# The z projection of a state-space block: two head groups in one product of 512 columns, in every second group

## The chip, the cores and the metric

The kernel runs on one core of one Trainium2 chip. The metric is the device time of one execution in microseconds (us), smaller is better. The times of this kernel of three runs lie within 0.13% of each other.

## The reference, cut to what matters

One transformer-like block on 512 tokens of width 1024, in float32. The input is normalised to `h`; one large projection `h @ w_in` gives the convolution branch, `z`, the state-space inputs `x`, `B`, `C`, the step sizes and the gates. What concerns us is the state-space branch, cut into 8 groups of 4 heads (256 of the 2048 columns of `z` belong to each group):

```
z   = proj[..., OFF_Z:OFF_XBC]                 # 2048 columns, 256 to a group
xbc = silu(causal_depthwise_conv(xbc, ...))    # x, B, C of every group
y   = ssd_chunked(x, dt, a, B, C, d_skip)      # the scan over chunks
y   = y * silu(z)
yg  = y by group;  yg = yg * rsqrt(mean(yg*yg) + eps)
ssm_out = (yg * norm_g) @ out_w
```

After it come the gates, an output projection, a residual, and a gated feed-forward layer.

## The kernel before, in words

Every float32 product is made in three passes. A factor is split into a rounded half `hi` and a remainder `lo`, and `mm3` (L160) issues hi*hi, hi*lo and lo*hi into one PSUM tile, so every logical product is three matmul instructions on TensorE (L162, L163, L164). The halves of `h` (`hhi`, `hlo`) stay in SBUF for the whole branch. The weights come in strips of 128 x 1024 values, in the order that the list `ORDER` writes out by hand (L84 to L97). A strip is loaded by SyncE's queue into one of five `raw` tiles, cast by ScalarE into `whi` (L129), and its remainder `wlo` is made either by VectorE (L134) or, for every second position in the list, by ScalarE's negated copy and an accumulating DMA that GpSimd issues (L131, L132). There are five `whi`/`wlo` slots; `w_get` asks for the strip that is needed and the three after it.

The branch runs in a loop over the groups g = 0..7 (L622 to L647). In a group the program issues: the two x products `proj_x` (24 matmuls of 512 columns each), then `s4(g-2)` (transposes of a finished y, tiles `pyT`, `yh`, `yl`) and `s1(g-1)` (transposes `pxT` and `pBT`, the product `pcb`), the B product, in odd groups from g = 3 half of the output projection `ssm_out` (`pso`), `s2(g-1)` (states `pSa`, `pSb`, and `yd`), the C product, the other half of `ssm_out`, `s3(g-1)`, and `proj_z(g)`. Then the decay table `L` of the next group is made: a DMA, a mask on GpSimd, 16 exponentials on ScalarE. In this text a group with even g is an even group, one with odd g an odd group; only odd groups (from 3) hold the 96 matmuls of `ssm_out`.

`s3(g)` is the step that uses z: it adds the parts of y (L558, L575), with the products `pYa`, `pYb` (L562) between them, multiplies by z (L577), squares on ScalarE (L582), takes the power on GpSimd (L170) and scales y on VectorE (L585). `s4(g)` one group later needs that result.

`proj_z` (L484) has the tokens as the stationary operand: for each of four chunks of 128 tokens and 8 steps in depth it issues three matmuls of 256 columns, 96 in all, two token chunks to one PSUM tile; ScalarE turns each full tile into z by one SiLU of 512 values to a partition (L496). The z of group 0 is made earlier together with the step sizes (`proj_z0`). z lives in one tile (tag `z`, one buffer), the projections share three PSUM tiles (tag `mm`).

VectorE also carries the long convolution of the other branch: 240 multiply-adds ("taps", L390), a share of which is released after each product (`conv_some`), never ahead of the last product issued. After the loop come the gates: `gate("gs", 0..4)` with `s4(6)`, `s1(7)`, `s2(7)`, `s3(7)`, `s4(7)` in between, each gate's sigmoid written to a tile of the ring `sg` (five buffers, idle during the group loop), and the last part of `ssm_out`.

The order on each engine is not quite that of the program: a planner at build time places each instruction by its own estimate of when operands and tiles come free, earlier program order first, so that a step whose operands it takes to be late is slipped between products of a later step. At run time every engine keeps the planned order.

Of the kernel before, what the change touches and what calls it, by code (L numbers as in the profile page):

```python
# [10 lines left out]
F32 = mybir.dt.float32  # L11
F32R = mybir.dt.float32r
BF16 = mybir.dt.bfloat16
AF = mybir.ActivationFunctionType
ALU = mybir.AluOpType
# [3 lines left out]
P = 128  # L19
T = 512  # L20
NT = T // P
D = 1024
NK = D // P
# [3 lines left out]
G = 8  # L27
HG = H // G
GW = DI // G
# [38 lines left out]
W_AHEAD = 3  # L68
# [7 lines left out]
DMA_EVERY = 2  # L76
DMA_FROM = 8
# [6 lines left out]
ORDER = []  # L84
# [3 lines left out]
for _g in range(G):  # L88
    _so = [("so", 2 * _g - 6 + _i) for _i in range(4)] if _g % 2 and _g > 1 else []
    ORDER += [("x", 2 * _g), ("x", 2 * _g + 1), ("B", _g)] + _so[:2] + [("C", _g)] + _so[2:]  # L90
    ORDER += [("z", 2 * _g), ("z", 2 * _g + 1)] if _g else []
ORDER += [("gs", _i) for _i in range(5)] + [("so", 2 * G - 4 + _i) for _i in range(4)]
ORDER += [("gs", _i) for _i in range(5, NK)] + [("gc", _i) for _i in range(NK)] + [("pw", _i) for _i in range(NK)]
ORDER += [("wo", _i) for _i in range(NK)]
ORDER += [("gu", 2 * _i) for _i in range(EARLY_U)] + [("gu", 2 * _i + 1) for _i in range(EARLY_U)]
ORDER += [("gu", _i) for _i in range(2 * EARLY_U, 2 * NF)]
ORDER += [("wd", _i) for _i in range(NF)]  # L97


def b3(ap, n):  # L100
# [5 lines left out]
def block_kernel(ctx: ExitStack, tc: tile.TileContext, x, xT, prm, hp, gp, w, out):  # L106
    nc = tc.nc
    act, dve, pe, pool = nc.scalar, nc.vector, nc.tensor, nc.gpsimd
# [11 lines left out]
    seq = {key: n for n, key in enumerate(ORDER)}  # L120
# [6 lines left out]
    def w_part(n, c):  # L127
        (hi, lo), src = split[n], raws[n]
        act.copy(hi[:, c], src[:, c])  # L129
        if n % DMA_EVERY == DMA_EVERY - 1 and DMA_FROM < n < seq[("gs", 0)]:  # L130
            act.activation(lo[:, c], hi[:, c].bitcast(F32), AF.Copy, scale=-1.0)  # L131
            pool.dma_start(lo[:, c], w[n][:, c].bitcast(F32R), accum_op=ALU.add)  # L132
        else:
            dve.tensor_tensor(out=lo[:, c], in0=src[:, c], in1=hi[:, c].bitcast(F32), op=ALU.subtract)  # L134
# [8 lines left out]
        if parts == 1:  # L143
            w_part(n, slice(0, 1024))

    def w_get(*key):

        n = seq[key]
        for m in range(n, n + W_AHEAD + 1):
            w_split(m)  # L150
        return split[n]

# [34 lines left out]
    hhi = hp_pool.tile([P, NK, T], F32R, tag="hi", name="hhi")  # L187
# [26 lines left out]
    def mm_tile(name):  # L214
        return mmp.tile([P, T], F32, tag="mm", name=name)
# [16 lines left out]
    ps = aux_tile("warm_ps")  # L232
# [163 lines left out]
    st = {}  # L396
# [84 lines left out]
        proj(ps, w_get(n, g))  # L481
        st[g][n] = conv4(ps, (2 if n == "B" else 3) * G + g, f"{n}{g}")

    def proj_z(g):  # L484
        z = ssd.tile([P, NT, GW], F32, tag="z", bufs=1, name=f"z{g}")
        ws = [w_get("z", 2 * g + j) for j in range(2)]
        for t2 in range(2):
            ps = mm_tile(f"pz{g}_{t2}")
            for t in range(2):
                tok = slice((2 * t2 + t) * P, (2 * t2 + t + 1) * P)  # L490
                o = ps[:, t * GW : (t + 1) * GW]
                for k in range(NK):
                    wh, wl = ws[k // 4]
                    c = slice((k % 4) * GW, (k % 4 + 1) * GW)
                    mm3(o, hhi[:, k, tok], hlo[:, k, tok], wh[:, c], wl[:, c], k == 0, k == NK - 1)
            act.activation(z[:, 2 * t2 : 2 * t2 + 2, :], ps.rearrange("p (a b) -> p a b", a=2), AF.Silu)  # L496
        st[g]["z"] = z

    def s1(g):
        s = st[g]  # L500
# [52 lines left out]
    def s3(g):  # L553
        s = st[g]
        hs = slice(HG * g, HG * (g + 1))
        y = s["y"]
        for n in range(2):
            dve.tensor_tensor(out=y[:, 2 * n : 2 * n + 2], in0=s["yd"][n], in1=y[:, 2 * n : 2 * n + 2], op=ALU.add)  # L558
        pa, pb = aux_tile(f"pYa{g}"), aux_tile(f"pYb{g}")
        pY = [None, pa[:, :GW], pa[:, GW:], pb[:, :GW]]  # L560
        for c in range(1, NT):
            pe.matmul(  # L562
                pY[c], s["C"][:, c * P : (c + 1) * P], s["prev"][:, c - 1].rearrange("p h d -> p (h d)"),
                start=True, stop=True,
            )
        yo = ssd.tile([P, NT - 1, HG, HD], F32, tag="yo", name=f"yo{g}")
        dve.tensor_tensor(
            out=yo[:, 0:2], in0=pa.rearrange("p (c h d) -> p c h d", c=2, h=HG),
            in1=b3(eacs[:, 1:3, hs], HD), op=ALU.mult,
        )  # L570
        dve.tensor_tensor(
            out=yo[:, 2], in0=pb[:, :GW].rearrange("p (h d) -> p h d", h=HG),
            in1=b3(eacs[:, 3, hs], HD), op=ALU.mult,
        )
        dve.tensor_tensor(out=y[:, 1:], in0=y[:, 1:], in1=yo, op=ALU.add)  # L575
        yz = y.rearrange("p c h d -> p c (h d)")
        dve.tensor_tensor(out=yz, in0=yz, in1=s["z"], op=ALU.mult)  # L577
        ss = ssd.tile([P, NT], F32, tag="ss", bufs=2, name=f"ss{g}")
        rs = ssd.tile([P, NT], F32, tag="rs", bufs=2, name=f"rs{g}")
        for c in range(NT):  # L580
            jk = ssd.tile([P, GW], F32, tag="jk", name="jk")
            act.activation(jk, yz[:, c, :], AF.Square, accum_out=ss[:, c : c + 1])  # L582
        power(rs, ss, 1.0 / GW, RMS_EPS, NT)
        for c in range(NT):
            dve.tensor_scalar(out=yz[:, c, :], in0=yz[:, c, :], scalar1=rs[:, c : c + 1], scalar2=None, op0=ALU.mult)  # L585
# [36 lines left out]
    for g in range(G):  # L622
        proj_x(g, 0)
        conv_some((TAPS[g] + 0) // 5)
        proj_x(g, 1)
        conv_some((TAPS[g] + 1) // 5)
        if g > 1:
            s4(g - 2)
        if g:
            s1(g - 1)  # L630
        st[g]["L"] = L.pop(g)
        proj_bc(g, "B")
        conv_some((TAPS[g] + 2) // 5)
        if g % 2 and g > 1:
            ssm_out((g - 3) // 2, (0, 1))
        if g:
            s2(g - 1)
        proj_bc(g, "C")
        conv_some((TAPS[g] + 3) // 5)
        if g % 2 and g > 1:  # L640
            ssm_out((g - 3) // 2, (2, 3))
        if g:
            s3(g - 1)
            proj_z(g)
        if g + 1 < G:
            L[g + 1] = make_L(g + 1)
        conv_some((TAPS[g] + 4) // 5)  # L647
# [441 lines left out]
def _layout(inp):  # L1089
# [11 lines left out]
    def piece(n, i):  # L1101
        if n == "gu":
            u, j = i // 2, i % 2
            o = (u % 2) * FF + (u // 2) * 2 * P
            one, two = [_feature_major(wgu, slice(o + q * P, o + (q + 1) * P)) for q in range(2)]
            return one if j == 0 else two
        if n in strips:
            a, o = strips[n]
            return _feature_major(a, slice(o + i * P, o + (i + 1) * P))
        if n == "zd":  # L1110
            a = zd[:, 3 * i : 3 * i + 3].reshape(P, -1)
            return np.pad(a, ((0, 0), (0, D - a.shape[1])))
        if n == "z":
            return zs[i // 2][:, (i % 2) * D : (i % 2 + 1) * D]
        if n == "so":
            a = so[(i // 4) * 512 : (i // 4 + 1) * 512, (i % 4) * 256 : (i % 4 + 1) * 256]
            return a.reshape(4, P, 256).transpose(1, 0, 2).reshape(P, -1)
        return rows[n][i * P : (i + 1) * P]
# [39 lines left out]
```

## Time and profile before

| what | value |
|---|---|
| median of 3 runs | 1085.08 us (1084.95 to 1086.33) |
| the profiled execution | 1086.54 us, of which the span from first to last instruction is 1084.8 us |
| TensorE clock granted | 0.996 of full speed |
| TensorE busy | 98% of the span |
| VectorE, ScalarE, GpSimd busy | 73%, 54%, 7% |

The profile holds one execution. A matmul's record is longer than the distance to the next one, since matmuls overlap: what a matmul costs is read from the distance between starts. A group of rows below is one view of the trace: a timeline row gives start and length in us, engine, line, operation, what it writes from what, and in brackets the idle time before it with what ended it; a windows row gives a stretch, its length, and each engine's busy time with the number of its instructions.

### The profile page before, as it was taken

What the parts mean: (1) busy time and instruction counts of PE and PEld (TensorE: products, weight loads), DVE (VectorE), ACT (ScalarE), POOL (GpSimd) and SP (SyncE); (2) the same over time, 40 slices, a digit from 0 to 9 for tenths busy, and PEclk for the clock granted to TensorE, in tenths of its full rate; (3) what the DMA queues carried; (4) which work ended last, traced back from release to release, by engine and by line L of the source; (5) the groups of instructions that cost most, each with busy time, mean ns of one, the idle gap of its engine ahead of it and who ended that gap; (6) DMA issues with size and microseconds to landing.
All of it is one profiled execution on the core that took longest, in us unless ns stands there. A gap on an engine that the chain in (4) does not pass through costs nothing.

```text
span 1084.8 us, 15679 instructions
## 1 busy us (share of the span) xinstructions
PE 1065.2 (98%) x6193; PEld 939.7 (87%) x6193; DVE 789.2 (73%) x1148; ACT 584.4 (54%) x955; POOL 79.0 (7%) x101
## 2 busy tenths in 40 slices
PE   8999999999999999999999999999999999999997
PEld 6888889988998899879888787888999999988886
DVE  6799995996698769696894365579988788643334
ACT  6657848595759464834323862466554554532222
POOL 2002001111111111100000000010000000000000
PEclk9999999999999999999999999999999999999999
DMA  7466543646535653452133222423332242353302
GB/s 276 124 175 216 153 120 98 176 117 194 136 98 143 169 136 98 117 137 78 40 99 119 75 98 78 175 98 117 117 137 98 80 135 98 118 192 100 98 1 78
DMA packets 37082, 132.98 MB, mean 123 GB/s; under 512 B 4368, under 2 KB 4624, under 8 KB 35984
## 3 DMA queue, kind: packets, MB, share of 16 engines
q1 hardware_dynamic: 28224, 97.31, 26.7%
q0 software_dynamic: 6048, 26.22, 11.3%
q10 hardware_dynamic: 2736, 8.46, 2.1%
q8 instruction: 48, 0.79, 0.3%
q14 instruction: 26, 0.21, 0.1%
HBM read 127.71 MB, written 4.26 MB: 122 GB/s over the span
## 4 chain that ended last, share of the span: by engine, by line
PE 83%; DVE 8%; ACT 3%; issue 1%; POOL 1%; DMA 0%; DVEq 0%; POOLq 0%; ACTq 0%
PE xy L162 5%; PE xy L164 5%; PE xy L163 5%; PE tm_wd L163 4%; PE tm_wd L164 4%; PE tm_wd L162 4%; PE pso L162 3%; PE pso L163 3%; PE pso L164 3%; PE yd L550 2%; PE pz L162 2%; PE pz L163 2%; PE pz L164 2%; PE px L162 2%; PE px L163 2%; PE px L164 2%
## 5 line engine op out<-in xcount | busy, mean ns | idle before, releaser
L129 ACT CAST whi<-raw 128x1024 fp32r<-128x1024 f32 (+1 forms) x134 | 137.8, 1035 | 211.1 <-PE pC L163 37.7
L390 DVE SCALAR_TENSOR_TENSOR a<-v,prm_t,a 128x485 f32<-128x485 f32 (+16 forms) x240 | 180.2, 755 | 4.2 <-ACT a L387 1.4
L134 DVE TENSOR_TENSOR wlo<-raw,whi 128x1024 fp32r<-128x1024 f32 (+1 forms) x100 | 119.3, 1198 | 52.7 <-ACT whi L129 52.5
L162 PE MATMUL pz<-whi,hhi 128*128 128x256 f32 (+1 forms) x256 | 74.5, 291 | 0.8 <-DVE sg L416 0.8
L163 PE MATMUL pz<-wlo,hhi 128*128 128x256 f32 (+1 forms) x256 | 73.1, 286 | 0.0
L164 PE MATMUL pz<-whi,hlo 128*128 128x256 f32 (+1 forms) x256 | 72.9, 285 | 0.0
L162 PE MATMUL tm_wd<-whi,fh 128*128 128x512 f32 x160 | 62.2, 389 | 0.0
L163 PE MATMUL tm_wd<-wlo,fh 128*128 128x512 f32 x160 | 62.2, 389 | 0.0
L164 PE MATMUL tm_wd<-whi,fl 128*128 128x512 f32 x160 | 62.2, 389 | 0.0
L821 DVE TENSOR_TENSOR wlo_g<-raw,whi_g 128x1024 fp32r<-128x1024 f32 x40 | 48.2, 1220 | 10.5 <-ACT whi_g L820 10.5
L820 ACT CAST whi_g<-raw 128x1024 fp32r<-128x1024 f32 x40 | 40.9, 1048 | 24.4 <-issue 10.2
L162 PE MATMUL pso<-yh,whi 128*128 128x512 f32 x128 | 50.2, 394 | 0.6 <-DVE B L467 0.6
L1031 DVE TENSOR_TENSOR fl<-f,fh 128x512 fp32r<-128x512 f32 x20 | 13.8, 691 | 50.3 <-ACT fh L1030 50.3
L164 PE MATMUL pso<-yh,wlo 128*128 128x512 f32 x128 | 50.1, 391 | 0.0
L132 POOL DMA_DIRECT2D wlo<-in_w x34 | 30.3, 891 | 271.9 <-ACT wlo L131 158.1
L162 PEld LDWEIGHTS pz<-whi,hhi 128*128 128x128 f32 x256 | 48.9, 191 | 1.3 <-DVE sg L416 1.0
L163 PE MATMUL pso<-yl,whi 128*128 128x512 f32 x128 | 50.0, 390 | 0.0
L162 PE MATMUL px<-hhi,whi 128*128 128x512 f32 x128 | 49.9, 390 | 0.0
L163 PE MATMUL px<-hlo,whi 128*128 128x512 f32 x128 | 49.9, 390 | 0.0
L164 PE MATMUL px<-hhi,wlo 128*128 128x512 f32 x128 | 49.8, 389 | 0.0
L163 PEld LDWEIGHTS pz<-wlo,hhi 128*128 128x128 f32 x256 | 48.9, 191 | 0.3
L164 PEld LDWEIGHTS pz<-whi,hlo 128*128 128x128 f32 x256 | 48.9, 191 | 0.2
(430 smaller groups left out, 3231.4 us busy)
## 6 DMA issues: line engine op xcount, KB each, us to landing
raw<-in_w SPq DMA_DIRECT2D x177, 512.0 KB, 3.7
wlo<-in_w POOLq DMA_DIRECT2D x34, 512.0 KB, 5.6
L<-scr POOLq DMA_DIRECT2D x8, 1024.0 KB, 5.2
xT<-in_xT SPq DMA_DIRECT2D x8, 256.0 KB, 5.9
xr<-in_x ACTq DMA_DIRECT2D x4, 512.0 KB, 4.7
x2d<-xr ACTq DMA_DIRECT2D x4, 512.0 KB, 2.6
x<-x2d ACTq DMA_DIRECT2D x1, 2048.0 KB, 10.9
raw<-in_w SPq DMA_DIRECT2D x4, 256.0 KB, 4.9
```

The lines of the kernel that those rows point to most:

```text
L129: act.copy(hi[:, c], src[:, c])
L132: pool.dma_start(lo[:, c], w[n][:, c].bitcast(F32R), accum_op=ALU.add)
L134: dve.tensor_tensor(out=lo[:, c], in0=src[:, c], in1=hi[:, c].bitcast(F32), op=ALU.subtract)
L162: mark["pe"] = pe.matmul(ps, lh, rh, start=start, stop=False, skip_group_check=more)
L163: pe.matmul(ps, lh, rl, start=False, stop=False, skip_group_check=more)
L164: pe.matmul(ps, ll, rh, start=False, stop=stop, skip_group_check=more)
L390: return dve.scalar_tensor_tensor(out=va[j][:, d:], in0=vs[j][:, : T - d], scalar=col("dw_w", j * KC + KC - 1 - d), in1=va[j][:, d:], op0= ...
L550: pe.matmul(yd[c // 2][:, c % 2, h, :], s["L"][:, h, c, :], s["xdt"][:, c, h, :], start=True, stop=True)
L820: a_ = act.copy(hi, src)
L821: d_ = dve.tensor_tensor(out=lo, in0=src, in1=hi.bitcast(F32), op=ALU.subtract)
L1031: dve.tensor_tensor(out=fs[k][1], in0=f32[:, k, :], in1=fs[k][0].bitcast(F32), op=ALU.subtract)
```

## The change

The z of group 1 is made as before (`proj_z1`). The z of groups 2 and 3, of 4 and 5, and of 6 and 7 are made together by `proj_zz(g)` in the even group of each pair: for each of four token chunks and 8 steps in depth three matmuls of 512 columns, 96 matmuls, one token chunk to a PSUM tile. Odd groups from 3 on have no z products any more. Each of the four PSUM tiles is read by two SiLUs of 256 columns: the first half into the z tile, the second into two tiles `zb` of the ring `sg`, where it stays until `s3(g+1)`; there the product with z is made in two halves. The weight strips are regrouped, four `zz` strips in a row after C of an even group (the number of strips is the same), each with columns of both groups. `w_get` takes a look-ahead that shrinks over the four strips, and the next strips are split between the last products of the block. A condition `after_zz` keeps the strip two positions after the last one of a block from the DMA route.

```
-    ORDER += [("z", 2 * _g), ("z", 2 * _g + 1)] if _g else []
+    ORDER += [("z", 0), ("z", 1)] if _g == 1 else [("zz", 2 * _g - 4 + _i) for _i in range(4)] if _g and _g % 2 == 0 else []
...
+ZZ_LAST = [("zz", 4 * _p + 3) for _p in range(G // 2 - 1)]
...
-        if n % DMA_EVERY == DMA_EVERY - 1 and DMA_FROM < n < seq[("gs", 0)]:
+        after_zz = n > 5 and ORDER[n - 2] in ZZ_LAST
+        if n % DMA_EVERY == DMA_EVERY - 1 and DMA_FROM < n < seq[("gs", 0)] and not after_zz:
...
-    def w_get(*key):
+    def w_get(*key, ahead=W_AHEAD):
...
-        for m in range(n, n + W_AHEAD + 1):
+        for m in range(n, n + ahead + 1):
...
+    def proj_zz(g):
+
+        z = ssd.tile([P, NT, GW], F32, tag="z", bufs=1, name=f"z{g}")
+        zb = [sg_tile(f"zb{g}_{i}").rearrange("p (a b) -> p a b", a=2) for i in range(2)]
+        n0 = seq[("zz", 2 * g - 4)]
+        ws = [w_get("zz", 2 * g - 4 + j, ahead=4 - j) for j in range(4)]
+        for t in range(NT):
+            tok = slice(t * P, (t + 1) * P)
+            ps = mm_tile(f"pz{g}_{t}")
+            for k in range(NK):
+                wh, wl = ws[k // 2]
+                c = slice((k % 2) * T, (k % 2 + 1) * T)
+                mm3(ps, hhi[:, k, tok], hlo[:, k, tok], wh[:, c], wl[:, c], k == 0, k == NK - 1)
+                if t == NT - 1 and k % 2:
+                    w_split(n0 + 5 + k // 2)
+            act.activation(z[:, t, :], ps[:, :GW], AF.Silu)
+            act.activation(zb[t // 2][:, t % 2, :], ps[:, GW:], AF.Silu)
         st[g]["z"] = z
+        st.setdefault(g + 1, {})["zb"] = zb
...
-        dve.tensor_tensor(out=yz, in0=yz, in1=s["z"], op=ALU.mult)
+        if "zb" in s:
+            for n, zb in enumerate(s["zb"]):
+                dve.tensor_tensor(out=yz[:, 2 * n : 2 * n + 2], in0=yz[:, 2 * n : 2 * n + 2], in1=zb, op=ALU.mult)
+        else:
+            dve.tensor_tensor(out=yz, in0=yz, in1=s["z"], op=ALU.mult)
...
             s3(g - 1)
-            proj_z(g)
+        if g == 1:
+            proj_z1()
+        if g and g % 2 == 0:
+            proj_zz(g)
```

## Rows read from the trace of the kernel before

**Rows 1.** Page: busy time, share of the span, instructions of an engine.
```profile
PE 1065.2 (98%) x6193; PEld 939.7 (87%) x6193; DVE 789.2 (73%) x1148; ACT 584.4 (54%) x955; POOL 79.0 (7%) x101
```

**Rows 2.** Page: the chain that ended last, by engine.
```profile
PE 83%; DVE 8%; ACT 3%; issue 1%; POOL 1%; DMA 0%; DVEq 0%; POOLq 0%; ACTq 0%
```

**Rows 3.** Windows, groups 2 to 7, each from its first x product.
```profile
179.16:221.71 42.55, 42.55 (x265) 38.22 (x264) 33.38 (x49) 31.08 (x50) 6.38 (x7) 1.00 0.39 113
221.71:286.81 65.10, 64.52 (x361) 56.20 (x360) 44.17 (x66) 50.84 (x91) 9.50 (x12) 1.00 0.58 154
286.81:329.40 42.59, 42.59 (x266) 38.24 (x264) 39.06 (x54) 23.73 (x34) 5.69 (x5) 1.00 0.44 124
329.40:395.03 65.63, 64.60 (x361) 56.20 (x360) 46.56 (x71) 44.63 (x79) 9.49 (x11) 1.00 0.57 145
395.03:437.62 42.59, 42.59 (x266) 38.24 (x264) 38.22 (x52) 22.15 (x33) 5.23 (x5) 1.00 0.43 122
437.62:504.11 66.49, 65.40 (x361) 56.03 (x360) 49.32 (x74) 33.08 (x58) 5.11 (x7) 1.00 0.42 112
```

**Rows 4.** Windows of the tile pz alone: z of groups 2, 5, all six.
```profile
209.18:221.71 12.53, 12.36 (x96) 11.87 (x96) 0.00 (x0) 0.00 (x0) 1.00 0.39 143
...
383.34:395.03 11.69, 11.69 (x96) 11.62 (x96) 0.00 (x0) 0.60 (x1) 1.00 0.49 121
...
sum 71.82, PE 71.49 PEld 70.21 DVE 0.00 ACT 1.78; mean PE 11.91 PEld 11.70 DVE 0.00 ACT 0.30
```

**Rows 5.** Timeline of PE, z of group 5: its 4th and 96th product.
```profile
383.88 0.28 PE L162 MATMUL pz<-whi,hhi 128*128 128x256 f32 x1
...
394.91 0.28 PE L164 MATMUL pz<-whi,hlo 128*128 128x256 f32 x1
```

**Rows 6.** Timeline of PE in the last projection, 36 steps from first to last.
```profile
999.82 0.39 PE L162 MATMUL tm_wd<-whi,fh 128*128 128x512 f32 x1
...
1007.98 0.39 PE L162 MATMUL tm_wd<-whi,fh 128*128 128x512 f32 x1
```

**Rows 7.** Timeline of PE: `pxT` at the start of groups 3, 5, 7.
```profile
239.73 0.39 PE L164 MATMUL pB<-hhi,wlo 128*128 128x512 f32 x1
240.70 0.66 PE L510 MATMUL pxT<-ident,x 128*128 128x128 f32 x4 [0.58 <-DVE yl L600]
...
348.38 0.66 PE L510 MATMUL pxT<-ident,x 128*128 128x128 f32 x4 [1.03 <-DVE yl L600]
...
458.03 0.66 PE L510 MATMUL pxT<-ident,x 128*128 128x128 f32 x4 [0.42 <-DVE yl L600]
```

**Rows 8.** Groups of instructions on ACT, 179 to 504 us: the evictions of z.
```profile
L496 ACT ACT_TABLE_LOAD x7 | 9.0, 1283 | 0.1
L496 ACT ACTIVATE z<-pz 128x512 f32<-128x512 f32 x12 | 7.1, 595 | 0.5 <-PE pz L164 0.4
```

**Rows 9.** The tile pz: evictions of 256 columns; count, min/median/max in ns.
```profile
L409 ACT ACTIVATE z<-pz x4: 363/383/386, 50.7 to 60.9; 128x256 f32<-128x256 f32 x4
```

**Rows 10.** Timelines of PE and DVE: `s3(2)` in group 3, its ends.
```profile
274.01 1.02 PE L562 MATMUL pYa<-prev,C 128*128 128x256 f32 x4
...
282.48 1.14 DVE L585 TENSOR_SCALAR y<-y,rs 128x256 f32<-128x256 f32 x4 [4.13 <-POOL rs L170]
```

**Rows 11.** Timelines of PE and DVE: `s3(6)` in group 7, its ends.
```profile
491.75 0.59 PE L562 MATMUL pYa<-prev,C 128*128 128x256 f32 x2
...
500.44 1.14 DVE L585 TENSOR_SCALAR y<-y,rs 128x256 f32<-128x256 f32 x4 [3.61 <-POOL rs L170]
```

**Rows 12.** Timelines in the gates: fourth gate's start, product with z, last transposes.
```profile
529.58 0.58 PE L162 MATMUL pgs<-hhi,whi 128*128 128x512 f32 x1
...
533.88 1.22 DVE L577 TENSOR_TENSOR y<-y,z 128x1024 f32<-128x1024 f32 x1
...
540.77 0.41 PE L598 MATMUL pyT<-ident,y 128*128 128x128 f32 x2
...
543.48 0.38 PE L598 MATMUL pyT<-ident,y 128*128 128x128 f32 x2
```

More of the change, by code (lines that the diff above doesn't have):

```diff
@@ L482, in proj_bc, with proj_z1 @@
         st[g][n] = conv4(ps, (2 if n == "B" else 3) * G + g, f"{n}{g}")
-    def proj_z(g):
-        z = ssd.tile([P, NT, GW], F32, tag="z", bufs=1, name=f"z{g}")
-        ws = [w_get("z", 2 * g + j) for j in range(2)]
+    def proj_z1():
+        z = ssd.tile([P, NT, GW], F32, tag="z", bufs=1, name="z1")
+        ws = [w_get("z", j) for j in range(2)]
         for t2 in range(2):
-            ps = mm_tile(f"pz{g}_{t2}")
+            ps = mm_tile(f"pz1_{t2}")
             for t in range(2):
@@ L496, in proj_z @@
             act.activation(z[:, 2 * t2 : 2 * t2 + 2, :], ps.rearrange("p (a b) -> p a b", a=2), AF.Silu)
+        st[1]["z"] = z
+    def proj_zz(g):
[14 more added lines that the diff above has]
+            act.activation(zb[t // 2][:, t % 2, :], ps[:, GW:], AF.Silu)
         st[g]["z"] = z
+        st.setdefault(g + 1, {})["zb"] = zb
     def s1(g):
@@ L1113, in piece @@
         if n == "z":
-            return zs[i // 2][:, (i % 2) * D : (i % 2 + 1) * D]
+            return zs[1][:, i * D : (i + 1) * D]
+        if n == "zz":
+            a = [zs[2 * (i // 4) + 2 + j].reshape(P, NK, GW)[:, 2 * (i % 4) : 2 * (i % 4) + 2] for j in range(2)]
+            return np.concatenate(a, axis=2).reshape(P, -1)
         if n == "so":
```

## The prediction

> **What bounds the kernel now.** I read the page first. TensorE is busy 98% of the span, VectorE 73% [rows 1], and the chain that ended last lies 83% on TensorE and 8% on VectorE [rows 2]. A busy share alone doesn't show who waits for whom, so I cut the branch into groups by windows [rows 3]. The reader is to see two things there. TensorE's busy time equals the length of the even groups and is about 1 us short of it in the odd ones: what shortens TensorE's own work here shortens the kernel, unless another engine steps in. And the load is uneven: VectorE is busy 39.06 of 42.59 us in group 4 (92%) and 46.56 of 65.63 us in group 5 (71%). Even groups are short, since only odd ones hold the output projection, and VectorE is nearly full in them. The waits of TensorE stand right behind them: at the start of each odd group `pxT` waits for VectorE's `yl`, the eviction of `pyT`, which frees its PSUM tile [rows 7].
>
> The change touches three terms: A, the z matmuls themselves; B, those waits at odd starts; C, waits that can arise because z no longer lies between `s3` and `s4` at the end of odd groups.
>
> **A: fewer, wider matmuls.** Removed: six blocks of 96 matmuls of 256 columns, in six windows of 71.82 us together, each from its first matmul to the next product's first [rows 4]. Steady spacing inside a block: 92 steps from the 4th to the 96th matmul take 394.91 - 383.88 = 11.03 us, 119.9 ns each [rows 5]. Added: three blocks of 96 matmuls of 512 columns with tokens stationary and weights moving. The feed-forward's last projection has that form: 36 steps take 8.16 us, 226.7 ns [rows 6]. So two old matmuls (239.8 ns) become one (226.7 ns), a gain of 13.1 ns, 288 times: 3.8 us. The rest of the old 71.82 us over 576 x 119.9 ns = 69.06 us is 2.76 us of starts and small waits. If none of it comes back the gain is 71.82 - 288 x 0.2267 = 6.5 us; if all of it does, 3.8 us. I give each new block the 0.3 us that an undisturbed old one has too (11.69 - 96 x 0.1199 = 0.18 us, rounded up, because four PSUM tiles are opened instead of two): 65.3 + 0.9 = 66.2 us. A = 71.8 - 66.2 = 5.6 us gained, between 3.8 and 6.5.
>
> The Trainium skill (TensorE: Matmul & The Clock Gate, section Back-to-back issue gap) speaks against this term: it gives an isolated matmul at full clock N/2.4 + 2.5 ns to the next, so that joining two of 256 saves 2.5 ns, 0.7 us in all as an estimate from that page. The spacings of 119.9 and 226.7 ns disagree with it: two of the narrow ones exceed a wide one by 13.1 ns.
>
> **B: waits at odd starts.** Group 3 has 0.58 us of idle time there, but its cost is the distance of 0.97 us from the last product less one step of 0.23 [rows 7]: 0.74 us. So an odd group without it takes 65.10 - 0.74 = 64.36 us; groups 5 and 7, with the same 361 matmuls, take 1.27 and 2.13 us more [rows 3]. Together 4.14 us. After the change an odd group starts behind a block of 22 us instead of 11.7 to 12.5, in which VectorE has nothing new to do but one subtraction. An even group is then 42.6 - 12.1 + 22.1 = 52.6 us long, an odd one 64.4 - 11.7 = 52.7. The list puts eight strips into each instead of six and ten, so about one VectorE subtraction of 1.2 us moves from odd to even: VectorE has 40 us of 52.6 in group 4 (77%), 48 of 52.7 in group 7 (91%, where the peak today is 92%). The nearest row for a start behind a long block is the even group of today, which shows no such wait [rows 3]. I take all of B: 4.1 us gained, bound below 0.
>
> **C: z gone from the end of odd groups.** `s3` ends an odd group, and `s4`, which needs its result, comes after the next two x products. Today z and x lie between (11.7 + 10.9 us), then x alone: 48 x 0.2267 = 10.9 us. In group 3 `s3` takes from 274.01 to 283.62 us, 9.6 us [rows 10]: it still fits, by 1.3 us plus the 1.1 us of its own matmuls, if VectorE is as free as in that row. It will be busier. For groups 4 and 6 I take 1.0 us each, near the waits at odd starts (0.74 to 2.13), bounds 0 and 2.13. Behind group 7 there is only one gate product, 5.4 us, before `s4(6)`, and the chain `s3(6)` took from 491.75 to 501.58, 9.8 us [rows 11]: 4.4 us are uncovered. The planner slips a step that is late between products: `s4(7)` today stands in four pairs of transposes from 540.77 to 543.48 us with output products between [rows 12], and TensorE lost little there. So I take 1.3 us, bounds 0 and 4.4. C = 3.3 us lost, bounds 0 and 8.7.
>
> **What costs nothing, and under which cover.** ScalarE: in the pairs, 12 SiLUs of 595 ns [rows 8] become 24 of about 383 ns [rows 9], 2.0 us more, and up to five more table loads each way at 1.28 us (12 blocks of evictions at worst against the 7 loads today), 13 us over three blocks; ScalarE is busy 22 to 31 us in an even group [rows 3], which becomes 10 us longer. Uncovered, a load delays the squares of `s3` by 1.28 us, and then `s4`. PSUM: a tile of the block is wanted again three tiles later, 10.9 us after it is full, against 0.8 us of SiLUs and two loads. VectorE's three products with z of 1.22 us [rows 12] are cut in two; even a whole 1.22 us more for each is 3.7 us of its free time. Weights: 36 strips and 34 DMA remainders stay as many; the fourth strip of a block needs the slot that B leaves, with the whole C product (5.4 us) for a cast and a subtraction of 1.0 + 1.2 us; the strips behind the block are split in its last quarter, the tightest (second x) with 4 + 5.4 us. On the queues two strip loads (SyncE) and one accumulating DMA (GpSimd, 7% busy [rows 1]) pass from the odd group to the even one before it, ahead of the next decay table; none is added. The condition `after_zz` meets even positions only, the DMA route takes odd ones: it changes nothing. One new wait: the fourth and fifth gates write `sg` tiles that `s3(7)`'s product must have read. The fourth gate's products start at 529.58 us and last 5.4 us, the product with z starts at 533.88 us and lasts 1.22 [rows 12]: both end at 535.1 us. If `s3(7)` comes later by the 4.4 us of C, the sigmoid waits as long, with the weight casts behind it in ScalarE's queue, whose strips are three products ahead.
>
> **Sum.** -5.6 - 4.1 + 3.3 = -6.4 us. Against the profiled execution, 1086.54 us, that is 1080.1 us; that execution lies 1.46 us above the median of the runs, 1085.08, so a median of 1078.7 us.
>
> **The rivals.** (1) No waits move in: C is 0, and A and B come in full: 1085.1 - 5.6 - 4.1 = 1075.4 us or less (6.5 + 4.1 gives 1074.5). For it: the even starts of today have none. Against: VectorE stays at 91% in odd groups. (2) The gain is eaten: VectorE's backlog only changes its place, so that B is regained at odd starts and lost again at even ones and in the gates, with C at 8.7: 1085.1 - 9.7 + 8.7 = 1084.1 us, which is no change; B = 0 with C = 3.3 gives 1082.8, at its edge. The page's rule would do the same through A: 0.7 instead of 5.6 us makes 1083.6; with the rows against it I give that way 2 of the 16 chances in 100 below. (3) Slower: the gates take the whole loss. VectorE is the pace from `s3(6)` to `s4(7)`; today z of group 7, 11.7 us of TensorE [rows 4], lies in front of the gates as cover while VectorE clears `s3(6)`. If none of the later products can be drawn forward, TensorE waits those 11.7 us at `s4(7)`, and with 2.7 us at the two even starts the time is 1085.1 - 9.7 + 14.4 = 1089.8 us. It decides as soon as the waits together pass 9.7 + 2.2 = 11.9 us. Against it: the planner fills, and the chain `s3(6)` asks for 4.4 us only.
>
> **How the numbers follow.** About 0.2% (2.2 us) is what a measurement of this kernel can tell from no change: 1082.9 to 1087.2 us counts as the same. Chances: the forecast (1076 to 1082.9 us) 0.59, rival 1 0.13, rival 2 0.16, rival 3 0.12. So faster 0.72, same 0.16, slower 0.12. The likeliest is 1078.7 us. The bounds of the terms reach from 1074.5 to 1085.1 - 3.8 + 8.7 = 1090 us; leaving out the tail of rival 1 and most of rival 3, the range is 1074.5 to 1086.0.
>
> **What would show it.** A: three z blocks of about 22.0 us, spacing 227 ns. B: `pxT` without idle time in groups 3, 5, 7. C: `pyT` of groups 4 and 6 following the x products with under 1 us lost, and from the end of `s3(6)` to the end of the gates no more than 2 us added. Groups of about 52 us each. The prediction is wrong if a z block is longer than 22.8 us (weights or evictions late), if VectorE's waits reappear in front of `pB` or `pC`, or if the output projection behind the gates starts late by more than the 4.4 us.

## The result, and the profile after

The changed kernel takes 1091.24 us (median of 17 runs, 1085.97 to 1093.09) against 1085.59 us of the kernel before in the same sitting. The ratio is 1.0047, with a 95% interval of 1.0037 to 1.0057. Median to median it is slower by 5.65 us, where 6.4 us less was forecast. The profiled execution took 1092.46 us, of which the span is 1090.7 us; it stands against the profiled 1086.54 us and span of 1084.8 us of before.

The page of the kernel after, busy time and the chain by engine:

```profile
PE 1065.8 (98%) x5905; PEld 926.7 (85%) x5905; DVE 790.0 (72%) x1151; ACT 592.7 (54%) x973; POOL 80.5 (7%) x101
...
PE 40%; DVE 5%; DMA 2%; issue 1%; ACT 1%; POOL 0%; DVEq 0%; POOLq 0%; ACTq 0%
```

Against [rows 1] there are 288 matmuls fewer, and TensorE is not busy for less: 1065.8 instead of 1065.2 us. What the wider products save must have come back inside TensorE's own busy time. The chain can't say where: it reaches back over only half of the span here. So the windows come next: the kernel after, groups 2 to 7 from the first x product of each, then the gates up to the first `pgc`. After the length come busy times of PE, PEld, DVE, ACT, POOL, then the granted clock, the DMA share and GB/s.

```profile
178.20:231.51 53.31, 53.24 (x266) 44.69 (x264) 37.44 (x56) 40.86 (x72) 8.10 (x9) 1.00 0.40 110
231.51:284.30 52.79, 52.79 (x265) 44.45 (x263) 38.39 (x53) 35.73 (x54) 6.93 (x7) 1.00 0.64 170
284.30:339.77 55.47, 53.86 (x266) 44.86 (x264) 43.56 (x66) 38.97 (x71) 8.55 (x9) 1.00 0.39 106
339.77:392.39 52.62, 52.62 (x264) 44.59 (x263) 42.44 (x59) 37.05 (x61) 7.06 (x7) 1.00 0.66 176
392.39:446.75 54.36, 53.60 (x266) 44.76 (x264) 42.41 (x65) 33.55 (x59) 7.69 (x9) 1.00 0.39 102
446.75:502.36 55.61, 53.50 (x265) 44.43 (x263) 44.39 (x62) 27.48 (x40) 2.67 (x3) 1.00 0.47 131
...
502.36:586.79 84.43, 81.09 (x380) 66.69 (x379) 68.80 (x102) 24.57 (x43) 2.87 (x4) 0.96 0.23 75
```

The gates of the kernel before, in the same cut:

```profile
504.11:581.16 77.05, 77.05 (x378) 63.98 (x376) 65.39 (x93) 24.40 (x36) 1.20 (x2) 1.00 0.28 89
```

The lengths of groups 2 to 7 add up to 324.95 us in [rows 3] and to 324.16 us here: the loop gained 0.79 us. The gates lost 7.38 us, which is more than the whole difference of the spans (5.9 us); the time before group 0 (115.78 to 114.81 us) and that behind the gates (503.6 to 503.9 us) make up the rest.

Inside the loop the reader can split the 0.79 us with the PE column. Its busy time falls from 322.25 to 319.61 us, 2.64 us. Length less busy time is what it waits: in even groups 0 before, 0.07 + 1.61 + 0.76 = 2.44 us after; in odd ones 0.58 + 1.03 + 1.09 = 2.70 us before, 2.11 us after, all of it in group 7. The z blocks of the kernel after, the tile `pz` alone:

```profile
208.24:231.51 23.27, 23.03 (x96) 17.93 (x96) 0.00 (x0) 2.08 (x6) 1.00 0.43 122
...
sum 69.53, PE 68.79 PEld 53.85 DVE 0.00 ACT 6.47; mean PE 22.93 PEld 17.95 DVE 0.00 ACT 2.16
```

**Where the gates lose.** Timeline of PE in the kernel after, around `s4(7)`:

```profile
544.13 0.41 PE L627 MATMUL pyT<-ident,y 128*128 128x128 f32 x2 [0.73 <-DVE y L614]
...
546.75 0.44 PE L627 MATMUL pyT<-ident,y 128*128 128x128 f32 x2 [0.47 <-DVE y L614]
547.86 0.96 PE L166 MATMUL pso<-yh,whi 128*128 128x512 f32 x3 [0.67 <-ACT yh L628]
549.82 0.79 PE L167 MATMUL pso<-yl,whi 128*128 128x512 f32 x1 [1.00 <-DVE yl L629]
...
550.84 0.63 PE L166 MATMUL pso<-yh,whi 128*128 128x512 f32 x1
...
555.84 0.39 PE L168 MATMUL pso<-yh,wlo 128*128 128x512 f32 x1
```

At 543 us the products that lie ready are used up, and TensorE takes the last group's y through transposes, `yh` and `yl` with nothing in between; before, output products stood between these transposes [rows 12]. Then something follows that no wait shows: from 549.82 us `pso` products are 0.43 us apart instead of 0.23. Windows of the same stretch; the clock is the third number from the end:

```profile
543.00:549.82 6.82, 3.48 (x17) 1.73 (x15) 6.19 (x12) 1.27 (x2) 0.59 (x1) 0.93 0.35 102
549.82:556.00 6.18, 6.18 (x15) 4.86 (x16) 6.01 (x9) 1.04 (x1) 0.00 (x0) 0.53 0.43 158
556.00:562.00 6.00, 6.00 (x31) 5.03 (x30) 3.72 (x6) 1.05 (x1) 0.00 (x0) 1.00 0.00 0
```

After 6.82 us in which TensorE was busy for 3.48, the granted clock is at its lower level, 1.2 instead of 2.4 GHz, for nearly 6 us, and then back. From 549.82 to 555.84 us there are 14 steps in 6.02 us; at 0.2267 us each [rows 6] they would take 3.17. So the clock costs 2.85 us and the waits 3.34 us (6.82 - 3.48), 6.2 of the 7.4 us; the remaining 1.2 us lies in the records of single products between the waits, each longer than its step in an unbroken row. The 17 runs agree with this, but don't show it by themselves: the two with a mean clock of 0.998 or more took 1085.97 and 1086.88 us, the fifteen at 0.992 to 0.995 took 1088.99 to 1093.09 us. A run's mean clock doesn't tell where the clock fell, and the kernel before spreads with it too: among its runs beside the first experiments, 1082.68 to 1083.63 us at 0.999 and 1085.39 to 1087.35 us at 0.995.

**Why `s4(7)` is late.** Timelines of DVE, ACT and POOL in the kernel after, `s3(6)` at the start of the gates:

```profile
505.56 1.22 DVE L606 TENSOR_TENSOR y<-y,z 128x1024 f32<-128x1024 f32 x1
...
513.90 1.13 DVE L614 TENSOR_SCALAR y<-y,rs 128x256 f32<-128x256 f32 x4
...
506.81 0.42 ACT L611 ACTIVATE jk<-y 128x256 f32<-128x256 f32 x1 [3.40 <-DVE y L606]
...
507.34 1.28 ACT L687 ACT_TABLE_LOAD   x1
508.64 0.69 ACT L687 ACTIVATE sgs<-pgs,prm_t 128x512 f32<-128x512 f32 x1
509.22 0.41 ACT L611 ACTIVATE jk<-y 128x256 f32<-128x256 f32 x1
...
510.39 1.05 ACT L132 CAST whi<-raw 128x1024 fp32r<-128x1024 f32 x1
511.33 0.42 ACT L611 ACTIVATE jk<-y 128x256 f32<-128x256 f32 x1
...
511.93 0.19 POOL L173 TENSOR_SCALAR pm<-ss 128x4 f32<-128x4 f32 x1 [34.92 <-ACT jk L611]
```

The same four squares in the kernel before:

```profile
496.86 0.42 ACT L582 ACTIVATE jk<-y 128x256 f32<-128x256 f32 x1 [4.10 <-DVE y L577]
...
498.48 0.42 ACT L582 ACTIVATE jk<-y 128x256 f32<-128x256 f32 x1
```

Before, the chain `s3(6)` ran under the z products of group 7, and the four squares followed each other in ScalarE's order: 2.2 us from the first to the power on GpSimd (499.09 us). Now it runs into the first gate. ScalarE works its planned order off, and there a sigmoid with its table load, a copy and a weight cast stand between the squares: 5.1 us, 506.81 to 511.93. `pYa` to the finished y takes 501.68 to 515.03 us, 13.35 us, and only 5.4 us of gate product cover it. TensorE does not wait at once: it draws the next gate products forward. The first `pyT` of group 6 comes 12.8 us behind the start of the gates (5.5 us before), the last `pyT` of group 7 44.6 us behind it (39.5 before), and the five gates are by then used up.

The slower squares are not what makes group 7 late: VectorE has other work while they run, and it starts the scalings of `s3(6)` at 513.90 us without idle time. What comes late is VectorE's own queue, which holds `s3(6)`, the taps, the weight remainders and `s3(7)` one behind the other. Windows from the first gate product to VectorE's first scaling of the y of group 7 (L585, now L614), in the kernel before and in the kernel after; DVE is the third busy time:

```profile
504.11:540.27 36.16, 36.16 (x192) 30.93 (x191) 33.25 (x48) 14.01 (x24) 1.20 (x2) 1.00 0.19 59
...
502.36:543.63 41.27, 41.04 (x211) 34.56 (x209) 38.69 (x60) 15.83 (x33) 2.87 (x4) 1.00 0.13 40
```

The stretch is 5.11 us longer, and VectorE is busy in it for 5.44 us more. About 4.0 us of that is its work for `s3(6)`, which lay ahead of the gates before [rows 11], under the z products of group 7; two more taps are 1.2 us.

### The profile page after: what moved, and what is told of

The parts are those of the page before. It is cut to its first block, busy times and chain, and to the rows that moved or that the text cites. A ratio compares the mean times of both kernels' runs of the same rounds, so it can differ in the third digit from the quotient of the medians.

```text
span 1090.7 us, 15138 instructions
## 1 busy us (share of the span) xinstructions
PE 1065.8 (98%) x5905; PEld 926.7 (85%) x5905; DVE 790.0 (72%) x1151; ACT 592.7 (54%) x973; POOL 80.5 (7%) x101
## 5 line engine op out<-in xcount | busy, mean ns | idle before, releaser
L166 PE MATMUL pz<-whi,hhi 128*128 128x512 f32 (+2 forms) x160 | 56.1, 357 | 0.8 <-DVE sg L420 0.8
L167 PE MATMUL pz<-wlo,hhi 128*128 128x512 f32 (+2 forms) x160 | 56.5, 353 | 0.3 <-DVE wlo L138 0.2
L168 PE MATMUL pz<-whi,hlo 128*128 128x512 f32 (+2 forms) x160 | 56.2, 352 | 0.0
L377 ACT ACTIVATE L<-L,nacs 128x128 f32<-128x128 f32 x128 | 41.0, 392 | 10.5 <-POOL L L371 10.2
L1062 ACT CAST fh<-f 128x512 fp32r<-128x512 f32 x20 | 12.4, 620 | 60.4 <-PE tm_wd L167 60.4
L471 DVE SCALAR_TENSOR_TENSOR x<-px,prm_t,x 128x511 f32<-128x511 f32 (+2 forms) x48 | 35.3, 744 | 6.1 <-ACT x L469 6.0
```

What stands on the lines that cost most here:

```text
L166: mark["pe"] = pe.matmul(ps, lh, rh, start=start, stop=False, skip_group_check=more)
L167: pe.matmul(ps, lh, rl, start=False, stop=False, skip_group_check=more)
L168: pe.matmul(ps, ll, rh, start=False, stop=stop, skip_group_check=more)
L377: act.activation(L[:, h, c, :], L[:, h, c, :], AF.Exp, bias=nacs[:, c, HG * g + h : HG * g + h + 1])
L471: dve.scalar_tensor_tensor(out=a[:, d:], in0=ps[:, : T - d], scalar=col("ssm_w", i * KS + KS - 1 - d), in1=a[:, d:], op0=ALU.mult, op1=ALU ...
```

## The experiments

All kernels compute the whole reference. The table holds what the sections below read; "2 to 5", "6, 7" and "gates" are lengths in us from windows cut as above, in one profiled execution each. The ratio is to the kernel before in the same sitting; the first two rows and the experiments come from four sittings, in which the median of the kernel before lay between 1085.19 and 1085.59 us.

| kernel | median us | ratio to before [95%] | groups 2 to 5 | groups 6, 7 | gates |
|---|---|---|---|---|---|
| before | 1085.59 | 1 | 215.87 | 109.08 | 77.05 |
| after | 1091.24 | 1.0047 [1.0037, 1.0057] | 214.19 | 109.97 | 84.43 |
| last pair apart | 1084.17 | 0.9992 [0.9981, 1.0004] | 213.99 | 110.81 | 77.01 |
| last pair only | 1092.08 | 1.0066 [1.0053, 1.0079] | 215.98 | 108.38 | 83.38 |
| sixth gate | 1084.26 | 0.9990 [0.9982, 0.9999] | 212.95 | 110.15 | 76.79 |
| before, sixth gate | 1085.65 | 1.0000 [0.9990, 1.0011] | 216.42 | 109.03 | 75.75 |
| moved, narrow | 1089.42 | 1.0046 [1.0030, 1.0061] | 214.94 | 108.19 | 83.32 |
| moved, narrow, sixth gate | 1083.08 | 0.9986 [0.9975, 0.9996] | 214.97 | 108.25 | 76.80 |
| exponentials first | 1084.00 | 0.9989 [0.9979, 1.0000] | 214.75 | 106.76 | 78.88 |
| exponentials first, sixth gate | 1081.98 | 0.9971 [0.9960, 0.9981] | 215.02 | 106.73 | 76.32 |
| own tiles | 1088.86 | 1.0034 [1.0020, 1.0048] | 213.13 | 110.40 | 82.91 |
| exponentials first in group 6 only, sixth gate | 1081.99 | 0.9971 [0.9960, 0.9983] | 213.52 | 107.57 | 76.32 |
| the last with own tiles | 1081.04 | 0.9959 [0.9944, 0.9973] | 213.57 | 107.30 | 76.32 |

**The last pair apart.** z of groups 6 and 7 is made singly, each at the end of its own group, as before; groups 2 and 4 keep their double blocks.

```
+PAIRS = [2, 4]
+ALONE = [1, 6, 7]
...
-    ORDER += [("z", 0), ("z", 1)] if _g == 1 else [("zz", 2 * _g - 4 + _i) for _i in range(4)] if _g and _g % 2 == 0 else []
+    ORDER += [("z", 2 * ALONE.index(_g) + _i) for _i in range(2)] if _g in ALONE else []
+    ORDER += [("zz", 4 * PAIRS.index(_g) + _i) for _i in range(4)] if _g in PAIRS else []
...
```

> The changed kernel, but z of groups 6 and 7 made one by one as before; pairs only in groups 2 and 4. Theory G (the loss sits in the gates: without the z products of group 7 as cover, the chain from s3(6) to s4(7) is late): the stretch from the first gate product to the first product of the second set of gates goes back from 84.4 to about 77 us with the clock full, and the time falls below the kernel before, to about 1084 us. Rival W (the joined blocks themselves and the order they force cost the time, in every pair): two thirds of the loss stay, 1089 us or more.

The gates of this kernel:

```profile
501.61:578.62 77.01, 77.01 (x377) 63.94 (x376) 65.39 (x93) 24.40 (x36) 1.20 (x2) 1.00 0.27 89
```

The loss in the gates is gone, waits and clock with it. Two thirds of the change remain, and the time is that of the kernel before within the interval: the first two pairs pay for nothing measurable. (Groups 2 to 5 give 1.9 us, but groups 6 and 7 take 1.7 us more than before.)

**The last pair only.** The reverse: only 6 and 7 are joined.

```
+PAIRS = [6]
+ALONE = [1, 2, 3, 4, 5]
...
```

> Only the pair of groups 6 and 7 is joined, all others as before. G: the gates lose what they lose in the changed kernel (stretch 83 to 85 us instead of 77), and groups 2 to 5 take the time of the kernel before: 1090 to 1093 us. Rival W (the loss needs several joined pairs, as lateness that adds up): a stretch below 80 us and 1087 us or less.

```profile
503.84:587.22 83.38, 80.98 (x381) 66.35 (x379) 68.73 (x102) 24.59 (x43) 2.88 (x4) 0.96 0.24 76
```

Most of the loss of the gates stands here: 6.3 of 7.4 us, with the clock at 0.96 as in the kernel after. The two runs together place the slowdown in the last pair, where z of group 7 is taken from between `s3(6)` and the gates; its width is tried below.

**A sixth gate as cover.** The kernel after, with one more gate product ahead of `s4(7)`; the product is done later otherwise, so no work is added.

```
-ORDER += [("gs", _i) for _i in range(5)] + [("so", 2 * G - 4 + _i) for _i in range(4)]
-ORDER += [("gs", _i) for _i in range(5, NK)] + [("gc", _i) for _i in range(NK)] + [("pw", _i) for _i in range(NK)]
+ORDER += [("gs", _i) for _i in range(6)] + [("so", 2 * G - 4 + _i) for _i in range(4)]
+ORDER += [("gs", _i) for _i in range(6, NK)] + [("gc", _i) for _i in range(NK)] + [("pw", _i) for _i in range(NK)]
...
     gate("gs", 4, sg_tile("sgs4"))
+    gate("gs", 5, va_tile("sgs5"))
     s4(G - 1)
...
```

> The changed kernel, with one more gate product (24 matmuls, 5.4 us of TensorE) placed ahead of s4(7) and the last output projection. G: it fills about the 4.9 us for which TensorE waits at s4(7), the clock does not fall behind it, and the stretch of the gates shrinks from 84.4 to 77 to 79 us: 1084 to 1087 us. Rival P (VectorE's total work is the pace of the gates, so a filler only moves the wait behind it): the stretch stays at 83 to 85 us, 1091 us.

```profile
502.39:579.18 76.79, 76.79 (x375) 64.19 (x374) 67.66 (x101) 24.60 (x43) 2.87 (x4) 1.00 0.25 83
```

One product of 5.4 us takes 7.6 us out of the gates and, across two sittings, 7.0 us off the median. No wait is left (the expectation put them at 4.9 us; the rows above give 3.34), and the clock stays at 1.00: so the fall of the clock went with the waits and was no property of the stretch. VectorE is as late as without the filler: its first scaling of group 7 comes 41.28 us behind the start of the gates. The sixth gate covers the lateness, it does not remove it.

**The control: before with the sixth gate.** The same edit in the kernel before.

> The kernel before with the same sixth gate product ahead of s4(7): the control for the filler. G: TensorE waits for nothing there, so nothing is gained, within 0.2% of the kernel before (1083.5 to 1087.8 us). Rival P, or a filler that is good for another reason: 3 us or more faster.

The ratio is 1.0000: what the sixth gate gives is given only where cover is missing.

**Moved, not widened.** The order of the change with the old products: two blocks of 256 columns one behind the other in the even group, the second z into `sg` tiles.

```
-    ORDER += [("z", 0), ("z", 1)] if _g == 1 else [("zz", 2 * _g - 4 + _i) for _i in range(4)] if _g and _g % 2 == 0 else []
+    ORDER += [("z", 2), ("z", 3)] if _g == 1 else [("z", 2 * _g + _i) for _i in range(4)] if _g and _g % 2 == 0 else []
...
-            proj_zz(g)
+            proj_z(g + 1, [sg_tile(f"zb{g}_{i}").rearrange("p (a b) -> p a b", a=2) for i in range(2)])
```

> The move without the widening: z of both groups of a pair made in the even group, but in two blocks of 96 matmuls of 256 columns, the second z kept in the sg tiles. G: the whole loss of the gates is there too (stretch 83 to 86 us), and the time is that of the changed kernel plus what the width saves, 2.3 to 3.8 us: 1093 to 1095 us. Rival W (wide blocks are bad for their waits): faster than the changed kernel, 1089 us or less.

Windows of `pz` alone, the three double blocks of this kernel, and then its group 7 and gates:

```profile
208.03:232.08 24.05, 23.88 (x192) 23.39 (x192) 0.00 (x0) 1.78 (x3) 1.00 0.64 182
...
sum 72.17, PE 71.67 PEld 70.19 DVE 0.00 ACT 5.35; mean PE 23.89 PEld 23.40 DVE 0.00 ACT 1.78
```

```profile
448.20:501.12 52.92, 52.89 (x265) 44.53 (x264) 44.37 (x62) 26.31 (x37) 1.80 (x2) 1.00 0.39 110
501.12:584.44 83.32, 79.98 (x381) 65.89 (x379) 68.70 (x102) 24.57 (x43) 2.87 (x4) 0.98 0.24 76
```

The move alone makes the kernel as slow as the whole change. The gates came as expected, the time did not: 1089.42 us lies 4 us below what G gave (and just above the 1089 us of rival W), so what the width saves does not show in the time. The width gains 72.17 - 69.53 = 2.64 us in the three blocks; but group 7 takes 52.92 us with narrow products and 55.61 us with wide ones, 2.69 us more.

**Moved, narrow, with the sixth gate** (the two edits above together): what is the width worth where the gates are covered?

> The move without the widening, with the filler: against the filler with wide products it gives what the width alone is worth. If the saving of the matmuls themselves arrives (70.7 - 68.1 us by the profiles): 2.6 us slower than the filler alone, about 1086.9 us. Rival N (what the width saves is lost again in group 7, where the narrow form has no wait): the same as the filler alone, 1084.3 us.

1083.08 us against 1084.26 us of the wide products with the same sixth gate, with intervals that overlap: nothing that can be measured, as rival N had it.

**Exponentials first.** What fills group 7? Timelines of ACT and DVE in the kernel after, behind the last z block:

```profile
449.85 1.28 ACT L519 ACT_TABLE_LOAD   x1
...
452.77 1.28 ACT L377 ACT_TABLE_LOAD   x1
454.06 2.45 ACT L377 ACTIVATE L<-L,nacs 128x128 f32<-128x128 f32 x8
456.42 0.80 ACT L391 ACTIVATE a<-v,prm_t 128x512 f32<-128x512 f32 x1
...
457.25 0.75 DVE L394 SCALAR_TENSOR_TENSOR a<-v,prm_t,a 128x511 f32<-128x511 f32 x1 [7.11 <-ACT a L391]
```

The last SiLUs and the exponentials of the next decay table alternate on ScalarE, each change with a load of 1.28 us. Behind them in its order stands the first tap `a`, on which VectorE waits 7.11 us; later in the group TensorE waits 1.52 us for VectorE's `xdec` and 0.56 us for its `B`. From group 2 to 7 the loads are 38, before 32. In this experiment, otherwise the kernel after, the next decay table is made ahead of the double block and its exponentials are put ahead of the block's SiLUs in ScalarE's order (groups 2, 4, 6).

```
+            not_before(act.activation(z[:, t, :], ps[:, :GW], AF.Silu), mark["exp"])
+            not_before(act.activation(zb[t // 2][:, t % 2, :], ps[:, GW:], AF.Silu), mark["exp"])
...
         if g and g % 2 == 0:
+            L[g + 1] = make_L(g + 1)
             proj_zz(g)
...
```

> The same order of exponentials in the changed kernel without the filler. G (the gates' loss comes from the missing cover of z of group 7, not from work that is late from the groups before): the stretch of the gates stays at 82 to 85 us, the time 2 to 4 us below the changed kernel, 1087 to 1089 us. Rival S2 (ScalarE's and VectorE's lateness is carried into the gates): the stretch falls below 80 us, 1083 us or less.

Its group 7 and its gates; and the first tap of its group 7 on DVE:

```profile
446.36:499.00 52.64, 52.64 (x264) 44.60 (x263) 45.09 (x63) 20.00 (x27) 2.67 (x3) 1.00 0.48 138
499.00:577.88 78.88, 77.98 (x380) 64.65 (x379) 68.11 (x101) 24.48 (x42) 2.94 (x4) 1.00 0.25 81
```

```profile
450.11 2.32 DVE L394 SCALAR_TENSOR_TENSOR a<-v,prm_t,a 128x511 f32<-128x511 f32 x3 [1.92 <-ACT a L391]
```

Group 7 loses its waits (55.61 to 52.64 us, busy throughout), with 22 table loads instead of 38. The gates were the surprise. I had held that they could not fall below some 82 us without another product as cover; they took 78.88 us without one, below the 80 us of rival S2 (its 1083 us were missed by 1 us), and that theory fell as it was put. What changes is VectorE's backlog. Its stretch from the first gate product to the first scaling of group 7, cut as above:

```profile
499.00:537.26 38.26, 38.26 (x200) 32.49 (x198) 35.38 (x54) 15.55 (x32) 2.94 (x4) 1.00 0.10 30
```

It is 3.01 us shorter than in the kernel after, with 3.31 us less of VectorE's work: three taps and one weight remainder fewer are left over from group 7, where VectorE now idles less. The power of `s3(7)` starts 36.4 us behind the start of the gates (535.44 us) instead of 39.5 (541.88), the waits there are 0.9 us, and the clock keeps its upper level. So lateness and cover are two sides of one sum: this edit makes VectorE less late, the sixth gate gives TensorE more to do meanwhile.

The same cut in the other profiles gives 36.14 and 36.16 us where z of group 7 lies ahead of the gates (last pair apart; before with the sixth gate), 41.28 us in the four that make it a group earlier with the old order on ScalarE (last pair only, sixth gate, both narrow ones), and 38.26 us in the other three with exponentials first; VectorE's busy times are 33.25 to 33.26, 38.69 to 38.70 and 35.38 us. Own tiles is the exception, 40.84 us with 36.91 busy: there VectorE waits 2.24 us for the power. No run took work from VectorE alone, so that its queue sets this time is read from the rows.

**Exponentials first, with the sixth gate.**

> The changed kernel with the sixth gate as filler and, in groups 2, 4 and 6, the 16 decay exponentials of the next group queued on ScalarE ahead of all SiLUs of the joined block, instead of between them. Theory S (the waits left in groups 6 and 7 come from ScalarE's queue: exponentials, SiLUs and the table loads between them stand in front of the first tap of a channel and of the x evictions, so VectorE stands idle in the block and is late in the next group): group 7 shrinks from 55.6 to 53 us or less, VectorE's idle 7.1 us in front of the tap fall below 3, fewer table loads; 3 us faster than the filler alone, about 1081 us. Rival V (VectorE's amount of work in odd groups sets it, whatever ScalarE does): group 7 stays at 55 us, 1084 us.

1081.98 us, faster than the kernel before by 0.19 to 0.40%. In the gates the two edits hardly add up (76.32 us against 76.79 and 78.88); group 7 keeps what the reorder gives (52.61 us). Groups 2 and 4 are longer by 3.5 and 0.8 us than in the kernel after, groups 3 and 5 shorter by 2.1 and 1.4: there the reorder only shifts time.

**Own tiles for the fourth and fifth gate.** The change put one new wait into the program: those two sigmoids write `sg` tiles that `s3(7)` must have read. Here they write to the z tile, idle by then, and their products with `so` are drawn ahead. The rest is the kernel after.

```
-    gate("gs", 3, sg_tile("sgs3"))
-    gate("gs", 4, sg_tile("sgs4"))
+    own = ssd.tile([P, 2, T], F32, tag="z", bufs=1, name="sgs34")
+    gate("gs", 3, own[:, 0, :])
+    gate("gs", 4, own[:, 1, :])
...
+    mul_s(3)
+    mul_s(4)
...
```

> The changed kernel, but the fourth and fifth gates write to the idle z tile instead of the sg tiles that hold the second z of group 6, so the new wait of their sigmoids for s3(7) is gone (their two products with the output parts move ahead of the pool's end). Theory G (the late chain s3(6) to s4(7) alone makes the wait): the stretch of the gates stays at 82 to 85 us and the time at 1089 to 1092 us. Rival T (the sigmoids that wait for the z tiles hold up ScalarE's queue and with it the squares of s3(7)): the stretch falls to 80 us or less, the time to 1087 us or less.

```profile
500.81:583.72 82.91, 79.81 (x380) 65.85 (x379) 68.58 (x102) 24.75 (x44) 2.44 (x4) 0.98 0.23 77
```

1.5 of the 7.4 us in the gates, and 2.4 us of the median, across two sittings: a small share, and far from the 80 us of rival T. TensorE still waits for the same y, `yh` and `yl` (3.10 us, 0.24 less), and the ratio stays above 1. The other 1.28 us are TensorE's busy time: its steps are 0.43 us apart for about 3 us here (548.76 to 551.75 us) instead of 6.

**Towards a better kernel.** First the reorder in group 6 alone, with the sixth gate; then with the own tiles too.

```
+        def late(ins):
+            if g == 6:
+                not_before(ins, mark["exp"])
...
+        if g == 6:
+            L[g + 1] = make_L(g + 1)
...
```

> The filler, with the exponentials ahead of the block's SiLUs in group 6 alone. S (what the order of ScalarE's queue gave lies in group 7, and in groups 2 and 4 it only made pyT or pxT late): groups 2 to 5 as with the filler alone (about 213 us), group 7 at 53 us: 1080 to 1082 us, not slower than with the order in all three groups. Rival: the gain needs all three, 1083 to 1084 us.

> The same with the fourth and fifth gates in the idle z tile. G: no change against the one before (within 1 us), since with the filler TensorE waits for nothing there. T: 1 to 2 us faster.

Group 7 and the gates of the last kernel:

```profile
447.27:498.80 51.53, 51.53 (x254) 43.56 (x253) 43.72 (x61) 18.83 (x25) 2.59 (x3) 1.00 0.50 142
498.80:575.12 76.32, 76.22 (x369) 63.59 (x368) 66.91 (x99) 24.48 (x43) 3.22 (x4) 1.00 0.26 83
```

Group 6 alone gives as much as all three (1081.99 us). With the own tiles it is 1081.04 us, ratio 0.9959 [0.9944, 0.9973], the fastest here and faster than both kernels; what the own tiles add to it is inside the intervals.

## Why the prediction was wrong

| term | forecast | measured | read from |
|---|---|---|---|
| A, wider products | -5.6 | -2.6 | PE busy, groups 2 to 7; the `pz` windows give -2.3 |
| B, waits in odd groups | -4.1 | -0.6 | PE length less busy |
| C, waits in groups 4 and 6 | +2.0 | +2.4 | the same, even groups |
| C, the gates | +1.3 | +7.4 | length of the gates |
| before group 0, behind the gates | 0 | -0.7 | the spans |
| sum | -6.4 | +5.9 | the spans |

**The step that failed is C at the gates**: "The planner slips a step that is late between products ... So I take 1.3 us, bounds 0 and 4.4." The gates lost 7.4 us. The step took the chain `s3(6)` at its old 9.8 us [rows 11], held it against the cover up to `s4(6)` only, and took slipping as free. At its new place the chain takes 13.35 us, and slipping was indeed free at `s4(6)`, where TensorE waits for nothing. But VectorE's work for `s3(6)` now stands in the gates in front of `s3(7)`, whose scalings come 5.1 us later with 5.4 us more of VectorE's work ahead of them; and each gate product drawn forward at `s4(6)` is missing at `s4(7)`, behind which nothing independent is left. Cover is a stock, and I looked for its end one step too early. That the place is right is shown by the two halves of the change (last pair apart, last pair only), that cover was missing by the sixth gate and its control; that VectorE's queue is what comes late is read from the traces. Rival 3 named the place, the outcome and the engine ("VectorE is the pace from `s3(6)` to `s4(7)`"); its price, 11.7 us of pure waiting, was not what came: 3.3 us of waits, 2.9 us of clock and 1.2 us of broken rows.

**The clock** was in no term. It turns a wait of 3 us into a loss of more than 6. The link to the waits is shown so far: the four profiles in which TensorE waits 2.5 to 3.4 us around `s4(7)` (the kernel after, last pair only, moved narrow, own tiles) show 0.96 to 0.98 in the gates, and the edits that take all or most of the waits away (last pair apart, sixth gate, exponentials first with 0.9 us left) show 1.00. Two of the 17 runs of the kernel after show almost no loss of clock; why is not known.

**A was mis-sized**, and lies below my own lower bound of 3.8. The step itself was right. Timeline of PE in the z block of group 2, kernel after, the unbroken row at its end:

```profile
222.67 0.39 PE L166 MATMUL pz<-whi,hhi 128*128 128x512 f32 x1
...
231.28 0.39 PE L168 MATMUL pz<-whi,hlo 128*128 128x512 f32 x1
```

38 steps take 8.61 us, 226.6 ns each, as forecast; in the moved narrow blocks 68 steps of 256 columns take 8.16 us, 120 ns each. So the 13.1 ns a pair did come, 3.8 us in all. The term that failed is "I give each new block the 0.3 us": over 288 steps of 0.2267 us the three blocks have 69.53 - 65.29 = 4.24 us of starts and small waits, where I put 0.9 and where the six old blocks had 2.76. In the block of group 2 they are 1.51 us: 0.19 at the first step, 0.43 us for a pair of `pYa` and 0.45 us for a pair of `pYb` that slip in (from 210.72 and 213.00 us), 0.35 us at 219.58 us for `wlo`. All three blocks (23.27, 22.90 and 23.36 us) are longer than the 22.8 us at which the prediction called itself wrong. The Trainium skill (TensorE: Matmul & The Clock Gate, Back-to-back issue gap) would have 2.5 ns a pair; the unbroken rows do not agree with that. What was left of A, 2.6 us, was lost again in group 7 (55.61 us against 52.92 with narrow blocks).

**B** came only in part: `pxT` has no idle time in groups 3, 5 and 7, as forecast. Groups 3 and 5 have no waits at all; in group 7 they came back in front of `pSa` and `pso` (not `pB` or `pC`, where the prediction's last part looked for them), through VectorE waiting on ScalarE's order, which the run with exponentials first shows. "VectorE has nothing new to do" was true (80% busy there, not the feared 91%), and beside the point: an engine that is not full can still be held up.

**C in groups 4 and 6** was right in size, but less than half of it is the wait that was meant, `pyT` behind `s3` (1.09 us in group 4). 0.52 us in group 4 and 0.58 us in group 6 are `pxT` waiting for `yl`: the waits of the odd starts, moved to even ones, as rival 2 had it; 0.18 us in group 6 is a wait of `pz` for `wlo`. The wait of `pyT` can be read in group 4, in timelines of ACT, DVE and PE of the kernel after:

```profile
285.08 2.46 ACT L377 ACTIVATE L<-L,nacs 128x128 f32<-128x128 f32 x8
287.43 2.00 ACT L132 CAST whi<-raw 128x1024 fp32r<-128x1024 f32 x2
...
288.51 1.22 DVE L138 TENSOR_TENSOR wlo<-raw,whi 128x1024 fp32r<-128x1024 f32 x1 [1.71 <-ACT whi L132]
289.65 1.22 DVE L606 TENSOR_TENSOR y<-y,z 128x1024 f32<-128x1024 f32 x1
...
296.64 1.46 PE L627 MATMUL pyT<-ident,y 128*128 128x128 f32 x8 [1.09 <-DVE y L614]
```

VectorE's product with z stands behind a weight remainder, that behind a cast, and the cast behind exponentials; at the end of the chain TensorE waits 1.09 us. This is argued from the timeline alone: the reorder that should have shortened it left group 4 at 55.8 us.

**What stays open**: whether fewer taps in the gates would mend the kernel as the sixth gate does, why two of 17 runs kept their clock, and what lengthens groups 2 and 4 when the exponentials go first.

## What to carry to other kernels

When a block is moved away from between a slow chain and its consumer, count the independent work behind the chain up to the last consumer, not to the first: whatever is drawn forward at the first is missing at the last. Time the chain at its new place, with what will stand between its instructions on each engine that works in order, and add up what it puts in front of the next chain on the busiest of them. And where a stage runs out of cover, one product that is due later anyway is the cheapest test and often the mend: here it was worth 7 us in the changed kernel and nothing in the one before.

## What the runs showed of the hardware

The granted clock fell to its lower level after 6.8 us in which TensorE was busy for 3.5 us, with no single wait longer than 1.00 us, and stayed there for some 6 us of unbroken products: 2.85 us lost with no wait in the record. Shorter idle times, 1.61 us spread over group 4 and 2.11 us over group 7, left it at 1.00.

A table load on ScalarE lasts 1.28 us in every row here, and the next instruction starts at once (507.34 + 1.28, next at 508.64 us). The Trainium skill (ScalarE: Activation LUTs, What ACT_TABLE_LOAD costs) adds a drain of 1.38 us to each change of table; no such gap shows here.
